# A hybrid decoder layer on one core: four large buffers instead of two, and another layout and loading order in the FFN's down phase

## The chip, the cores and the metric

The kernel runs on one core of one Trainium2 chip. The metric is the device time of one execution in microseconds (us); lower is better. Profile lines come from one profiled execution; engines are PE (matmul), PEld (its weight loads), DVE (VectorE), ACT (ScalarE), POOL (GpSimd) and SP (SyncE). DMAs are issued by SP, POOL and, for one small store, ACT, each into a queue of its own.

## The reference

One layer of a decoder on x of 1024 tokens by 1024 channels, all float32. Two token mixers run beside each other, then a gated FFN with a causal convolution of three taps. Cut to what matters:

```python
h = layer_norm(x, ln_in_g, ln_in_b)
u_glu, z, xbc, dt_raw, gate_a, gate_b = split_in(h @ w_in)
y_a = conformer_branch(u_glu, ...)       # GLU, causal conv of 31 taps, LN, silu, @ w_conv_out
y_b = ssd_branch(z, xbc, dt_raw, ...)    # conv of 4 taps, Mamba-2 SSD in chunks of 128, gated RMS norm, @ w_ssm_out
mix = (sigmoid(gate_a) * y_a + sigmoid(gate_b) * y_b) @ w_o
h = layer_norm(DN_ALPHA * h + mix, ln1_g, ln1_b)
u = causal_dwconv(h @ w_up, dw_w, dw_b)  # 1024 -> 2 * 2816 channels, 3 taps
gate, val = split(u)
ffn = (silu(gate) * val) @ w_down        # 2816 -> 1024
h = layer_norm(DN_ALPHA * h + ffn, ln2_g, ln2_b)
```

## The kernel before, in words

**Precision.** Every large matmul works on operands split in two: a high half (ACT casts to fp32r, a reduced-precision float that PE takes at full rate) and a low half (DVE subtracts the high half from the original). A product is three matmuls, high x high, high x low and low x high, which stand in `mm3` at L183, L184 and L185. So each weight tile of 128 x 1024 costs one ACT cast and one DVE subtraction before PE can use it: L149 and L154 in the mixers, L851/L852 in the up phase, L1116/L1117 in the down phase.

**Stages.** The tokens are done in two halves of 512 for the mixers (projections, the convolution of 31 taps as scalar_tensor_tensor operations on DVE at L466, the SSD chunks, the combination, the output projection). In the mixers' SSD branch a group's root mean square is found by a chain: a small PE product (L590), ACT's square root (L598), DVE's reciprocal (L599), a store to `nrm_scr` and a load back as `rstd`, and DVE's scaling with it (L605). Then comes the FFN over all 1024 tokens:

- *Up phase.* For each of 22 column blocks j, the 1024 x 1024 activations and the weights are taken as 2 x 2 blocks and multiplied with seven block products instead of eight (Strassen's scheme in Winograd's form), whose operands are called b11, b21, b22 and t1 to t4. `up_first` does b11 and b21; `up_rest` does t2, t3, t1, t4 and b22, brings the results from PSUM into `ug` and `uv` (ACT copies at L980, L983 and L988, DVE at L984 and L986; `fug`, `fuv` in the trace), runs the convolution of three taps (ACT L994, twice DVE L998 for each of gate and value), the silu (L1008) and the gating (L1009), and stores blocks and their differences to `b11_scr`, `b2_scr`, `t32_scr` and `t1_scr` (POOL, L1019 to L1027; the trace calls b11's and b2's both b_scr).
- *Down phase.* `down` is again seven block products, p = 0 to 6, each of 11 steps k. A step, `load(p, k)`, brings an activation block (SP, L1079) and a weight block (SP, L1082) into one raw buffer `dr` of five in a ring, for some products a further block `other` (POOL, L1088; `do` in the trace), forms the sums with a DVE addition (`add`, L1051: for p = 0 the sum is kept as `c3[k]`, for p = 1 as `c4[k]`), casts (L1116) and subtracts (L1117) into a weight buffer `w_dn`, and PE does 12 matmuls into four accumulators. After a product's last step its four accumulators are added to the residual rows `rs` (L1134 and its neighbours); when a row tile has both halves, its layer norm follows (L224, L238, L240, L244, L247) and its store. The last product runs its last eight steps one row tile after the other, so that the norms overlap it.

**Buffers.** SBUF is given out by pools with fixed numbers of buffers; an operation that needs a buffer waits until the last reader of its former content is done. Pool `big` has two buffers of 32 KiB per partition; they hold, one after the other, the transposed activations with their halves: `hT`, `yT`, `mixT`, then `h1b1` (b11 and b21) and `h1b2` (t3 and t4). In the down phase one holds the eight residual row tiles (`rows`) and the other the eleven c3 blocks; the weights of the last four steps of the last product (`last`) are built in c3's buffer at the end. The four `other` buffers are two pairs from two pools, taken in turn.

**Order.** The order of the instructions on each engine is set when the kernel is built: the Tile scheduler plays the program through with its own costs and gives each engine its list; `high_priority` moves a piece ahead, `issue_after` adds an order without a wait. On the chip each engine runs its list in order, and an instruction that waits holds up all behind it. An edit in one place can thus move instructions far from it.

## Time and profile before

| What | Value |
|---|---|
| runs | 1958.3, 1958.61, 1961.29 us; median 1958.61 |
| profiled execution | 1960.26 us, of which the span of the core's work is 1958.4 |
| TensorE's clock, mean over the span | 0.997 of full |
| busy, share of span | PE 99%, DVE 82%, PEld 80%, ACT 55%, POOL 11% |
| HBM traffic | 192 GB/s over the span |

PE's busy time says which engine sets the pace; since it is at 99%, one looks for the few places where PE waits, and at what released it. A line "PE ... [1.14 <-ACT w_dn L1116]" says that PE was idle for 1.14 us before that instruction and that ACT's instruction of line 1116 ended the wait. The table of stretches gives each engine's busy time between two times of the span, with the clock granted to PE, the share of time in which the 16 DMA engines were busy, and the rate. The chain is followed back from the last instruction to what released each step. For DMAs, "us to landing" counts from issue.

### The profile page before, as it was taken

Reading aid. Unit: us, or ns where it says so; the run is one execution under the profiler, and the core shown is the slowest. Engines: PE = TensorE matmul, PEld = TensorE weight load, DVE = VectorE, ACT = ScalarE, POOL = GpSimd, SP = SyncE. Lnnn points to the kernel's source line nnn. Section 1 sums busy time; section 2 is a strip of 40 time slices with the busy share of each in tenths; the row PEclk is TensorE's granted clock in tenths of the full one; section 3 lists DMA queues with packets and bytes.
Section 4 is the critical chain, followed back from the end, with each engine's and each line's share of the span. In section 5 each row is a group of like instructions: output and inputs, shape, how many; then the busy total and the mean of one; then the engine's idle time right before and its main releaser. Section 6 shows DMA issues by size and latency. Waiting matters only on the chain.

```text
span 1958.4 us, 25837 instructions
## 1 busy us (share of the span) xinstructions
PE 1929.1 (99%) x9453; PEld 1574.9 (80%) x9453; DVE 1599.8 (82%) x2224; ACT 1081.2 (55%) x1615; POOL 218.9 (11%) x258
## 2 busy tenths in 40 slices
PE   9999999999999999999999999999999999989997
PEld 8888878788788788888878888888888888867886
DVE  7599999999786538898999546587788888879778
ACT  4676767653263266777765435365555555544432
POOL 0001010112210001111112140010000000121010
PEclk9999999999999999999999999999999999999999
DMA  7645555447355565556545644566455455588673
GB/s 270 224 166 205 174 202 185 159 171 245 116 188 212 198 214 175 205 181 208 176 159 168 216 145 134 188 237 230 163 167 189 166 188 178 198 301 276 195 230 127
DMA packets 127648, 378.36 MB, mean 193 GB/s; under 512 B 15104, under 2 KB 15648, under 8 KB 127520
## 3 DMA queue, kind: packets, MB, share of 16 engines
q1 hardware_dynamic: 107424, 318.48, 48.2%
q0 software_dynamic: 13760, 46.69, 6.9%
q10 hardware_dynamic: 6336, 11.54, 1.6%
q8 instruction: 74, 1.21, 0.3%
q14 instruction: 54, 0.44, 0.1%
HBM read 289.99 MB, written 86.65 MB: 192 GB/s over the span
## 4 chain that ended last, share of the span: by engine, by line
PE 60%; DVE 10%; DMA 3%; ACT 2%; issue 2%; DVEq 0%; SPq 0%; ACTq 0%
PE acc L185 13%; PE acc L184 13%; PE acc L183 13%; PE sm L184 6%; PE sm L185 6%; PE sm L183 6%; DVE c L466 4%; DMA dr<-wdown 1%; DVE x L421 1%; DMA st_wo<-wo 1%; DMA b_scr<-fo 1%; PE sm L551 1%; PE sm L554 0%; DVE m L546 0%; ACT m L519 0%
## 5 line engine op out<-in xcount | busy, mean ns | idle before, releaser
L183 PE MATMUL acc<-hT,w_c 128*128 128x512 f32 x1000 | 391.2, 391 | 0.0
L185 PE MATMUL acc<-hT,w_c 128*128 128x512 f32 x1000 | 391.1, 391 | 0.0
L184 PE MATMUL acc<-hT,w_c 128*128 128x512 f32 x1000 | 391.0, 391 | 0.0
L466 DVE SCALAR_TENSOR_TENSOR c<-v,pc,c 128x512 f32<-128x512 f32 x480 | 369.7, 798 | 7.3 <-ACT c L455 4.5
L183 PEld LDWEIGHTS acc<-hT,w_c 128*128 128x128 f32 x1000 | 187.8, 188 | 40.6 <-issue 1.9
L185 PEld LDWEIGHTS acc<-hT,w_c 128*128 128x128 f32 x1000 | 187.8, 188 | 40.0 <-issue 1.5
L184 PEld LDWEIGHTS acc<-hT,w_c 128*128 128x128 f32 x1000 | 187.8, 188 | 39.5 <-issue 1.1
L149 ACT CAST w_c<-st_c 128x1024 fp32r<-128x1024 f32 x128 | 133.9, 1046 | 127.6 <-PE acc L185 100.6
L530 POOL TENSOR_TENSOR ce<-ce,xbc 128x1024 f32<-128x1024 f32 x28 | 82.2, 2936 | 681.7 <-ACT ce L529 681.7
L1116 ACT CAST w_dn<-dr 128x1024 fp32r<-128x1024 f32 (+1 forms) x73 | 68.6, 944 | 88.3 <-DMA dr<-wdown 36.7
L183 PE MATMUL sm<-h1s,w_s 128*128 128x512 f32 x264 | 102.7, 389 | 0.0
L184 PE MATMUL sm<-h1s,w_s 128*128 128x512 f32 x264 | 102.7, 389 | 0.0
L185 PE MATMUL sm<-h1s,w_s 128*128 128x512 f32 x264 | 102.2, 389 | 0.0
L519 ACT ACTIVATE m<-ab,acs 128x128 f32<-128x128 f32 x256 | 78.3, 390 | 37.7 <-PE sm L551 36.6
L154 DVE TENSOR_TENSOR w_c<-st_c,w_c 128x1024 fp32r<-128x1024 f32 x64 | 79.4, 1243 | 22.3 <-ACT w_c L149 17.1
L1117 DVE TENSOR_TENSOR w_dn<-dr,w_dn 128x1024 fp32r<-128x1024 f32 (+1 forms) x73 | 78.9, 1092 | 6.1 <-ACT w_dn L1116 6.1
L421 DVE SCALAR_TENSOR_TENSOR x<-u,pc,x 128x512 f32<-128x512 f32 x96 | 78.8, 835 | 3.9 <-ACT x L419 3.8
L185 PE MATMUL acc<-h1b,w_ue 128*128 128x512 f32 x176 | 68.8, 394 | 0.3 <-DVE w_ue L154 0.3
L183 PE MATMUL acc<-h1b,w_ue 128*128 128x512 f32 x176 | 68.7, 390 | 0.0
L184 PE MATMUL acc<-h1b,w_ue 128*128 128x512 f32 x176 | 68.5, 389 | 0.0
L183 PE MATMUL sm<-h1b,w_s 128*128 128x512 f32 x176 | 68.5, 389 | 0.0
L184 PE MATMUL sm<-h1b,w_s 128*128 128x512 f32 x176 | 68.5, 389 | 0.0
(325 smaller groups left out, 4547.3 us busy)
## 6 DMA issues: line engine op xcount, KB each, us to landing
st_c<-wcol SPq DMA_DIRECT2D x128, 512.0 KB, 4.4
low_scr<-w_c SPq DMA_DIRECT2D x64, 512.0 KB, 2.9
w_c<-low_scr SPq DMA_DIRECT2D x64, 512.0 KB, 4.4
ab<-acs_scr SPq DMA_DIRECT2D x32, 512.0 KB, 4.1
dr<-wdown SPq DMA_DIRECT2D x55, 256.0 KB, 5.2
st_wo<-wo SPq DMA_DIRECT2D x24, 512.0 KB, 4.5
st_ue<-wup SPq DMA_DIRECT2D x22, 512.0 KB, 3.6
first_scr<-first ACTq DMA_DIRECT2D x44, 256.0 KB, 3.0
```

The source lines that it names most:

```text
L149: casts.append(A.copy(w[:, 0, :], st))
L154: V.tensor_tensor(out=w[:, 1, :], in0=st, in1=w[:, 0, :].bitcast(F32), op=ALU.subtract)
L183: TE.matmul(ps, wa(0), xa(0), start=start, stop=False, skip_group_check=more)
L184: TE.matmul(ps, wa(0), xa(1), start=False, stop=False, skip_group_check=more)
L185: TE.matmul(ps, wa(1), xa(0), start=False, stop=stop, skip_group_check=more)
L421: V.scalar_tensor_tensor(out=o, in0=u[:, k : k + HALF], scalar=pc[:, wc + k : wc + k + 1], in1=o, op0=ALU.mult, op1=ALU.add,)
L466: V.scalar_tensor_tensor(out=accs[i], in0=v[:, k : k + HALF], scalar=pc[:, wc + k : wc + k + 1], in1=accs[i], op0=ALU.mult, op1=ALU.add,)
L519: A.activation(out=m[:, h, :], in_=ab[:, h, :], func=AF.Relu, scale=-1.0, bias=acs[:, c, 8 * g + h : 8 * g + h + 1],)
L530: G.tensor_tensor(out=ce, in0=ce, in1=CT[:, cs].unsqueeze(1).to_broadcast([P, 8, P]), op=ALU.mult)
L551: TE.matmul(o, xs[:, h * HP : (h + 1) * HP], m[:, h, :], start=True, stop=first)
L1116: A.copy(w[:, 0, cs], src)
L1117: V.tensor_tensor(out=w[:, 1, cs], in0=src, in1=w[:, 0, cs].bitcast(F32), op=ALU.subtract)
```

## The change

Nothing is computed in another way, and PE's matmuls stay the same in number. What changes is where things lie and when they are loaded:

1. Pool `big` has four buffers of 16 KiB instead of two of 32; an activation's high and low half are two tiles (`Parts` picks one by the first index).
2. In `down`, the four hold c3[0..7]; rows 0 to 3; c3[8..10] with c4[7] and c4[8]; and rows 4 to 7. Before, c3 took all of the buffer that `h1b2` leaves; now c3[0..7] and rows 0 to 3 take the two that `h1b1` leaves.
3. Rows 0 to 3 are loaded at the start of the phase; rows 4 to 7 in the third product (p = 2), behind the last `other` of the second; the norm's gain and offset rows (`ln2_g`, `ln2_b`) in the fifth (p = 4).
4. The four `other` buffers all come from one pool, and the last store of b11 is issued behind the fourth `other`. The weight buffer of step 3 is taken early (`first_own`).
5. The weights of the last four steps of the last product are built in the fifth product, one each at k = 3, 5, 7 and 9, into c3's two buffers.

```diff
-    big = ctx.enter_context(tc.tile_pool(name="big", bufs=2))
+    big = ctx.enter_context(tc.tile_pool(name="big", bufs=4))
...
     def big_tile(name):
-        return big.tile([P, 2, KD, HALF], F32R, tag="big", name=name)
+        return Parts(big.tile([P, KD, HALF], F32R, tag="big", name=f"{name}_{i}") for i in "hl")
...
-            G.dma_start(b11_scr[j], ov[:, early])
+            stores.append(G.dma_start(b11_scr[j], ov[:, early]))
...
-        rows, kept = flat_big("rows"), flat_big("c3")
-        c3 = [kept[:, k * HALF : (k + 1) * HALF] for k in range(NK)]
-        c4 = [dp.tile([P, HALF], F32, name=f"c4_{k}") for k in range(NK - 1)]
+        c3, rows03 = blocks(flat_big("c3")), flat_big("rows03")
+        more_c3 = blocks(flat_big("more_c3"))
+        c3 += more_c3[:3]
+        rows47 = flat_big("rows47")
+        c4 = [
+            more_c3[k - 4] if 7 <= k < 9 else dp.tile([P, HALF], F32, name=f"c4_{k}")
+            for k in range(NK - 1)
+        ]
...
-        for t in range(8):
-            G.dma_start(rs[t], h1_scr[t * P : (t + 1) * P, :])
-        g, b = (row(dp, w, D, n, eng=G) for w, n in ((RW_2G, "ln2_g"), (RW_2B, "ln2_b")))
+        first_own = dp.tile([P, 2, D], F32R, tag="w", bufs=3, name="w_dn_own")
+
+        def load_row(t):
+            i = G.dma_start(rs[t], h1_scr[t * P : (t + 1) * P, :])
+            if t >= 4:
+                issue_after(i, others[-1])
+
+        for t in range(4):
+            load_row(t)
...
-                    n_other += 1
-                    pl, tag = ((dp, "other"), (upp, "s"))[n_other % 2]
-                    other = pl.tile([P, HALF], F32, tag=tag, bufs=2, name=f"do{p}_{k}")
-                    G.dma_start(other, o_of)
+                    other = dp.tile([P, HALF], F32, tag="other", bufs=4, name=f"do{p}_{k}")
+                    others.append(G.dma_start(other, o_of))
+                    if len(others) == 4:
+                        issue_after(stores[-1], others[-1])
...
                     if not last:
-                        last.append(big_tile("last").rearrange("p i k t -> p (i k t)"))
-                    w = last[0][:, (k - NK + 4) * 2 * D : (k - NK + 5) * 2 * D]
-                    w = w.rearrange("p (i n) -> p i n", i=2)
+                        w = flat_big(f"last{k}", F32R)
+                        w = w.rearrange("p (j i n) -> p j i n", j=2, i=2)
+                        last.extend(w[:, j] for j in range(2))
+                    kept[k] = w = last.pop(0)
...
                 w = load(p, k)
+                if p == 2 and k % 2 and k < 8:
+                    load_row(4 + k // 2)
+                elif p == 4 and k == 1:
+                    load_norm()
+                elif p == 4 and k % 2:
+                    load(6, NK - 4 + k // 2 - 1)
...
-            ws = {k: load(p, k) for k in range(end, NK)}
+            ws = {k: kept.get(k) or load(p, k) for k in range(end, NK)}
```

Lines are shifted in the changed kernel: L1116/L1117 are L1148/L1149, L1051 is L1081, L1046 is L1066, L1088 is L1116, L994 is L1002, L998 is L1006, L984 and L986 are L992 and L994, L1009 is L1017, L1134 is L1166, L244 and L247 are L250 and L253, L599 is L605, L605 is L611.

The instructions move at four places. First POOL at the turn from the up to the down phase, before (`rows` are the residual rows, `do_` the `other` blocks of p = 0, b_scr and t_scr the stores of the up phase):

```order
175 L1046 DMA rows<-h_scr 128x1024 x8
176 L971 MEMSET fuv_14026 128x2
...
180 L1026 DMA t_scr_180<-fo_13955 128x1024
181 L1088 DMA do_0_14268<-wdown 128x512
182 L971 MEMSET fuv_14130 128x2
183 L1019 DMA b_scr_148<-fo_14104 128x512
184 L1088 DMA do_1_14289<-wdown 128x512
185 L1088 DMA do_3_14331<-wdown 128x512
186 L220 DMA ln_g<-prow 128x1024
187 L220 DMA ln_b<-prow 128x1024
188 L1088 DMA do_2_14310<-wdown 128x512
```

and the same place of the changed kernel:

```order
175 L1066 DMA rows_14243<-h_scr 128x1024 x4
176 L979 MEMSET fuv_14036 128x2
...
180 L1034 DMA t_scr_180<-fo_13965 128x1024
181 L979 MEMSET fuv_14140 128x2
182 L1116 DMA do_0_14273<-wdown 128x512
183 L1116 DMA do_1_14294<-wdown 128x512
184 L1116 DMA do_2_14315<-wdown 128x512
185 L1116 DMA do_3_14336<-wdown 128x512
186 L1027 DMA b_scr_148<-fo_14114 128x512
187 L1116 DMA do_4_14356<-wdown 128x512
```

Four row loads instead of eight stand at the start, the four first `other` loads are together and ahead of the last b11 store, and the norm's rows are gone from here.

DVE over the same turn, before: the last taps of the FFN's convolution (L998), the first weights' low halves (L1117) and the first sums (L1051).

```order
1726 L1117 TENSOR_TENSOR w_dn_0_14271<-dr_14265,w_dn_0_14271 128x1024
1727 L998 SCALAR_TENSOR_TENSOR fo_14100<-fug_14025,pc,fo_14100 128x1024
...
1729 L998 SCALAR_TENSOR_TENSOR fo_14100<-fug_14025,pc,fo_14100 128x1024
1730 L1117 TENSOR_TENSOR w_dn_1_14292<-dr_14286,w_dn_1_14292 128x1024
1731 L998 SCALAR_TENSOR_TENSOR fo_14104<-fuv_14026,pc,fo_14104 128x1024
1732 L984 TENSOR_TENSOR fuv_14130<-sm_14137,fuv_14130 128x512
1733 L1009 SCALAR_TENSOR_TENSOR fo_14104<-fo_14104,pc,fo_14100 128x1024
1734 L1117 TENSOR_TENSOR w_dn_2_14313<-dr_14307,w_dn_2_14313 128x1024
...
1737 L1051 TENSOR_TENSOR c_14233<-dr_14265,do_0_14268 128x512
```

and of the changed kernel:

```order
1726 L1006 SCALAR_TENSOR_TENSOR fo_14110<-fug_14035,pc,fo_14110 128x1024
1727 L1149 TENSOR_TENSOR w_dn_0_14276<-dr_14270,w_dn_0_14276 128x1024
...
1729 L1006 SCALAR_TENSOR_TENSOR fo_14114<-fuv_14036,pc,fo_14114 128x1024 x2
1730 L992 TENSOR_TENSOR fuv_14140<-sm_14147,fuv_14140 128x512
1731 L1017 SCALAR_TENSOR_TENSOR fo_14114<-fo_14114,pc,fo_14110 128x1024
1732 L1149 TENSOR_TENSOR w_dn_1_14297<-dr_14291,w_dn_1_14297 128x1024
1733 L1149 TENSOR_TENSOR w_dn_2_14318<-dr_14312,w_dn_2_14318 128x1024
1734 L1149 TENSOR_TENSOR w_dn_own<-dr_14333,w_dn_own 128x1024
1735 L1081 TENSOR_TENSOR c_14242<-dr_14270,do_0_14273 128x512
```

The first weight's low half now stands behind the first tap, the second's behind all taps and the gating, and the first sum follows the fourth low half. On PE the up phase's last products, b22 and t4 of block 21, stand behind the second weight's twelve matmuls before; now b22 stands ahead of the second weight's four high matmuls, and t4 between these and its other eight.

DVE at the end of the program, before (row tiles 6 and 7 of the layer norm):

```order
1972 L238 BN_AGGR mv_f_15908<-st_f_14251 128x2
1973 L1134 SCALAR_TENSOR_TENSOR rows<-rows,acc_14227 128x512
1974 L244 SCALAR_TENSOR_TENSOR rows<-rows,mv_f_15908,ln_g 128x512 x2
1975 L240 RECIPROCAL rs_f_15909<-rs_f_15909 128x1
1976 L224 BN_STATS st_f_14252<-rows 128x6
1977 L247 SCALAR_TENSOR_TENSOR rows<-rows,rs_f_15909,ln_b 128x512 x2
```

and of the changed kernel:

```order
1970 L244 BN_AGGR mv_f_15919<-st_f_14261 128x2
1971 L250 SCALAR_TENSOR_TENSOR rows_14245<-rows_14245,mv_f_15919,ln_g 128x512 x2
1972 L246 RECIPROCAL rs_f_15920<-rs_f_15920 128x1
1973 L1166 SCALAR_TENSOR_TENSOR rows_14245<-rows_14245,acc_14237 128x512
1974 L253 SCALAR_TENSOR_TENSOR rows_14245<-rows_14245,rs_f_15920,ln_b 128x512 x2
1975 L230 BN_STATS st_f_14262<-rows_14245 128x6
```

The pair that subtracts row tile 6's mean (L244, now L250) moves ahead of the addition of the last accumulator.

And DVE in the first half's mixers, before (convolution taps, weights' low halves w_c_46 and w_c_47, the reciprocal of the fourth group):

```order
571 L154 TENSOR_TENSOR w_c_46_4391<-st_c_46_4389,w_c_46_4391 128x1024
572 L466 SCALAR_TENSOR_TENSOR c_6_4222<-v_6_3506,pc,c_6_4222 128x512
573 L599 RECIPROCAL rows_3_4204<-rows_3_4204 128x128
574 L466 SCALAR_TENSOR_TENSOR c_7_4224<-v_7_3574,pc,c_7_4224 128x512
...
578 L154 TENSOR_TENSOR w_c_47_4425<-st_c_47_4423,w_c_47_4425 128x1024
```

and of the changed kernel:

```order
567 L472 SCALAR_TENSOR_TENSOR c_7_4227<-v_7_3576,pc,c_7_4227 128x512
568 L605 RECIPROCAL rows_3_4207<-rows_3_4207 128x128
569 L472 SCALAR_TENSOR_TENSOR c_6_4225<-v_6_3508,pc,c_6_4225 128x512
570 L472 SCALAR_TENSOR_TENSOR c_7_4227<-v_7_3576,pc,c_7_4227 128x512
571 L160 TENSOR_TENSOR w_c_46_4394<-st_c_46_4392,w_c_46_4394 128x1024
```

The reciprocal stands five rows earlier, ahead of w_c_46's low half instead of behind it, by the scheduler's choice alone; the source there is the same.

More of the change, by code (lines that the diff above doesn't have):

```diff
@@ L52, with __getitem__ @@
 CT_N = 72
+class Parts(tuple):
+    def __getitem__(self, at):
+        return tuple.__getitem__(self, at[1])[(at[0], *at[2:])]
 @with_exitstack
@@ L957, in up_weights @@
         return w24, w10, w3
+    stores = []
     def up_rest(upp, bl, j, before):
@@ L1034, in down, with flat_big, blocks, load_norm @@
         X, Y = [bank(1) for _ in range(4)], [bank(0) for _ in range(4)]
[L1036 to L1041 removed]
+        def flat_big(name, dtype=F32):
+            t = big.tile([P, KD, HALF], dtype, tag="big", name=name)
+            return t.rearrange("p k t -> p (k t)")
+        def blocks(t):
+            return [t[:, k * HALF : (k + 1) * HALF] for k in range(KD)]
+        c3, rows03 = blocks(flat_big("c3")), flat_big("rows03")
[6 more added lines that the diff above has]
+        ]
         c4.append(upp.tile([P, HALF], F32, tag="s3", name="c4_last"))
[L1043 removed]
+        rs = [r[:, t * D : (t + 1) * D] for r in (rows03, rows47) for t in range(4)]
         sts = [dp.tile([P, 2, 6], F32, name=f"st_f{t}") for t in range(8)]
[L1045 to L1047 removed]
+        g, b = (dp.tile([P, D], F32, name=n) for n in ("ln2_g", "ln2_b"))
+        first_own = dp.tile([P, 2, D], F32R, tag="w", bufs=3, name="w_dn_own")
[5 more added lines that the diff above has]
+            load_row(t)
+        def load_norm():
+            for r, start in ((g, RW_2G), (b, RW_2B)):
+                i = G.dma_start(r, prow[start : start + D].partition_broadcast(P))
+                issue_after(i, others[-1])
         E, L = slice(0, HALF), slice(HALF, D)
@@ L1051, in add @@
             V.tensor_tensor(out=dst, in0=x, in1=y, op=ALU.add)
[L1053 removed]
+        n_steps, n_raw = 0, 0
         def raw(name):
@@ L1059, in raw @@
             return pl.tile([P, D], F32, tag=tag, bufs=bufs, name=f"{name}_{n_raw}")
-        last = []
+        last, others, kept = [], [], {}
         def load(p, k):
-            nonlocal n_steps, n_other
+            nonlocal n_steps
             a11, a21, a12, a22 = (wdown[h * NK + k, :, cs] for h in range(2) for cs in (E, L))
```

7 lines of the change are left out of this document (2 added, 5 removed).

## The prediction

> **What bounds the kernel now.** I read the table of engines first, then PE's waits by stretch, PE's timeline where it waits, the chain that ended last around those places, and a table of stretches.
>
> ```profile
> PE 1929.1 (99%) x9453; PEld 1574.9 (80%) x9453; DVE 1599.8 (82%) x2224; ACT 1081.2 (55%) x1615; POOL 218.9 (11%) x258
> ```
>
> TensorE is the bound: of a span of 1958.4 us it is idle 1958.4 - 1929.1 = 29.3 us. The change takes away no matmul, so it can win only from these 29.3 us, or add to them. PE's waits in 500:520, 990:1000 and 1700:1800 (us in total, times, longest):
>
> ```profile
> PE acc L185 <- DVE w_gb L154: 4.2, 1, 4.2
> ...
> PE sm L551 <- DVE m L546: 2.5, 1, 2.5
> ...
> PE acc L184 <- DVE w_dn L1117: 3.7, 3, 1.6
> PE sm L184 <- DVE w_dn L1117: 2.1, 1, 2.1
> PE acc L183 <- ACT w_dn L1116: 2.1, 2, 1.1
> ```
>
> So 4.2 us stand in the first half's mixers and 7.9 us at the start of the down phase, all waits for weights being prepared. PE's timeline there (start, duration, idle time before in brackets):
>
> ```profile
> 1726.62 1.19 PE L183 MATMUL acc<-w_dn 128*128 128x512 f32 x4 [1.14 <-ACT w_dn L1116]
> 1729.09 0.50 PE L184 MATMUL acc<-w_dn 128*128 128x512 f32 x1 [1.28 <-DVE w_dn L1117]
> ...
> 1745.74 1.20 PE L183 MATMUL acc<-w_dn 128*128 128x512 f32 x4 [0.92 <-ACT w_dn L1116]
> ...
> 1754.61 0.50 PE L184 MATMUL acc<-w_dn 128*128 128x512 f32 x1 [1.62 <-DVE w_dn L1117]
> ...
> 1761.18 0.50 PE L184 MATMUL acc<-w_dn 128*128 128x512 f32 x1 [0.80 <-DVE w_dn L1117]
> ...
> 1774.70 0.50 PE L184 MATMUL sm<-w_dn 128*128 128x512 f32 x1 [2.09 <-DVE w_dn L1117]
> ```
>
> They add to 7.85 us. What they hang on, in the chain (start, us, what):
>
> ```profile
> 1710.47 12.35 DMA b_scr<-fo
> ...
> 1727.90 1.15 DVE w_dn L1117
> ...
> 1736.44 0.24 PE sm L185
> 1736.70 0.70 DVE c L1051
> 1737.84 6.74 DMA dr<-wdown
> ...
> 1754.95 11.95 DMA dr<-wdown
> ```
>
> Two causes show. A store of the convolved block takes 12.35 us beside the burst of eight row loads; the FFN's last DVE work starts late behind it, and the low half of the second weight ends only at 1729.05. Then the first sum into c3 waits for the last up product (PE's end at 1736.68), since c3 lies in that product's operand; the raw buffers that feed the sums are held till then, SP's next load goes out at 1737.8 and lands at 1744.6, and the gaps from 1745 on follow. The stretches (length, then busy us of PE, PEld, DVE, ACT, POOL, then PE's granted clock, DMA share, GB/s):
>
> ```profile
> 425.00:510.00 85.00, 80.78 (x383) 65.26 (x382) 82.80 (x109) 34.62 (x46) 18.89 (x17) 0.99 0.56 189
> ...
> 512.00:514.00 2.00, 2.00 (x6) 1.63 (x5) 1.97 (x4) 0.00 (x0) 0.00 (x0) 0.50 0.98 350
> ...
> 996.00:998.00 2.00, 0.86 (x16) 0.89 (x18) 2.00 (x4) 1.98 (x3) 0.00 (x0) 1.00 0.48 193
> ...
> 1725.00:1800.00 75.00, 67.10 (x287) 52.64 (x286) 67.05 (x82) 31.38 (x32) 17.01 (x32) 1.00 0.83 289
> 1797.00:1858.00 61.00, 61.00 (x270) 50.50 (x270) 47.33 (x66) 29.21 (x40) 3.29 (x6) 1.00 0.63 202
> 1858.00:1918.00 60.00, 60.00 (x266) 49.69 (x265) 45.46 (x58) 24.62 (x29) 6.56 (x12) 1.00 0.68 216
> 1920.00:1940.00 20.00, 20.00 (x90) 16.57 (x89) 20.00 (x40) 5.67 (x11) 0.00 (x0) 1.00 0.29 107
> 1948.00:1958.00 10.00, 0.17 (x1) 0.00 (x0) 7.21 (x15) 0.59 (x2) 0.00 (x0) 0.68 0.43 158
> ```
>
> A matmul costs 60.00/266 = 0.226 us; the twelve of one down step about 2.72. After 1800 PE has no idle time until its last matmul at 1948.17; from there DVE finishes alone.
>
> **The change part by part.** *Four row loads ahead of the store, and the first weights (1.14 + 1.28).* ACT's timeline of before:
>
> ```profile
> 1718.31 0.58 ACT L988 COPY fug<-sm 128x512 f32<-128x512 f32 x1
> ...
> 1722.98 1.15 ACT L994 ACTIVATE fo<-fug,pc 128x1024 f32<-128x1024 f32 x1 [1.85 <-DMA b_scr<-fo]
> ```
>
> The scaling L994 needs `fug`, there at 1718.9, and a buffer that the store gives back at 1722.8. With four rows the burst is 2 MiB instead of 4, and half of it has gone when the store is issued; if the store lands in six us (the row load on SP's queue beside it, shown below, took 6.4), L994 starts at 1718.9, four us sooner, and DVE's work behind it too. PE's order now puts the b22 and t4 products between the first weight and the lows of the second: 24 matmuls, 5.4 us of cover. That low half goes behind one tap, one subtraction and one multiplication more on DVE, about 3.0 together: 1729.05 - 4 + 3 = 1728. PE asks for it at 1725.5 + 0.7 + 5.4 + 0.9 = 1732.5. The 0.7 is a new wait that I expect: b22 adds to a bank that ACT copies first, about 1726. What speaks against it: the first weight's cast and low half now stand behind L994 and the first tap. If the store stays at 12.35, the cast ends at 1722.98 + 2.1 = 1725.1 and the low at 1726.6, where PE wants them at 1722.6 and 1723.5: 3.1 us of new waits in place of 2.42. Gain 1.7, bounds 2.42 and -0.7.
>
> *c3 in the early buffers (0.92 + 1.62 + 0.80 + 2.09 = 5.43).* c3[0..7] now lies where h1b1 was, whose last product is long over, and four `other` loads are issued back to back ahead of the last b11 store. The first sum is then bounded by DVE's own queue: three lows from 1728, about 1732 to 1733 in place of 1736.7, so SP's ring turns 4 us sooner: w_dn_5 could be cast at about 1744.6 - 4 = 1740.6, and PE wants it, without the earlier gaps, at about 1742. Also 3 MiB leave this stretch (rows 4 to 7, and two norm rows of 0.5 MiB each), where the DMA engines are busy 0.83 of the time and a load took 11.95. What is late next is DVE: it has 67.05 us to do here, and if the stretch shrinks by 7 us that is 67.05 of 68. The low halves that come closest have some 1 to 2 us of slack in my walk through the new order, so I leave 0.6 of gaps. Gain 4.8; bounds 5.43, and zero if DVE's queue holds the sums as long as c3's buffer did.
>
> Together 6.5, bounds -0.7 and 7.85.
>
> *The loop of four `other` buffers* replaces two pairs that were taken in turn, four in all as well. Its DMA rows in 1700:1800 (KB each, median us to landing):
>
> ```profile
> do<-wdown POOLq DMA_DIRECT2D x26, 256.0 KB, 5.7
> ...
> rows<-h_scr POOLq DMA_DIRECT2D x8, 512.0 KB, 10.4
> ...
> fug<-first_scr SPq DMA_DIRECT2D x1, 256.0 KB, 6.4
> ```
>
> At 5.7, with the sum's 0.70 and about 0.5 for the issue, a buffer turns in 6.9, four give one per 1.73 us: below the 2.72 of a step. Cost 0.
>
> *Rows 4 to 7, norm rows.* They go out on POOL's queue behind the last `other` of the second product. POOL is busy 3.29 of 61 us in 1797:1858 and no row is wanted before the last product. The DMA engines moved 202 GB/s there; 3 MiB over 61 us add 52, giving 254, less than the 289 that 1725:1800 carried. Cost 0, up to 4 if the burst delays SP's loads (a rival below).
>
> *Last weights built in the fifth product.* Four weights, each two half-casts on ACT and two half-lows on DVE (about 0.6 each) and one load on SP, move there from the last product. DVE is busy 45.46 of 60 us in 1858:1918; plus 4.8 makes 50.3. Covered by PE, cost 0; without that cover, 4.8 at most. The place they leave is DVE's full stretch 1920:1940.
>
> *The tail.* DVE's rows after PE's end:
>
> ```profile
> 1948.21 0.69 DVE L1134 SCALAR_TENSOR_TENSOR rows<-rows,acc 128x512 f32<-128x512 f32 x1
> 1948.81 1.41 DVE L244 SCALAR_TENSOR_TENSOR rows<-rows,mv_f,ln_g 128x512 f32<-128x512 f32 x2
> ...
> 1953.88 1.41 DVE L247 SCALAR_TENSOR_TENSOR rows<-rows,rs_f,ln_b 128x512 f32<-128x512 f32 x2
> ```
>
> The L244 pair of row 6 stands ahead of the last L1134 in the new order: 1950.14 - 1948.81 = 1.33 us less to do after PE. DVE has room to do it, since the last weights' lows are gone. Gain 1.33, bounds 1.33 and 0.
>
> *The gap at 509.* The scheduler also moves a square-root chain of the first half:
>
> ```profile
> 461.21 0.95 DVE L599 RECIPROCAL rows<-rows 128x128 f32<-128x128 f32 x1
> ...
> 472.73 2.74 DVE L605 SCALAR_TENSOR_TENSOR x<-x,pc,rstd 128x512 f32<-128x512 f32 x4 [1.77 <-DMA rstd<-nrm_scr]
> ...
> 509.67 0.80 PE L185 MATMUL acc<-hT,w_gb 128*128 128x512 f32 x1 [4.22 <-DVE w_gb L154]
> 510.26 0.63 PE L183 MATMUL acc<-hT,w_gb 128*128 128x512 f32 x1
> 510.69 0.63 PE L184 MATMUL acc<-hT,w_gb 128*128 128x512 f32 x1
> ```
>
> DVE is busy 82.80 of 85 us in 425:510; the 1.77 is most of what it idles, and everything behind it up to PE's wait is DVE's queue. The reciprocal now stands one weight low and several taps sooner, about 3 us, more than 1.77, and what it goes through (a store and a load back) shifts along. So DVE no longer waits, and PE's gap falls to 4.22 - 1.77 = 2.45. After the gap, 512:514 still ran at clock 0.50; matmuls start 0.43 us apart instead of 0.226, 11 of them up to 514.4: 2.2 us. After the 2.5 us gap at 997, the clock was 1.00. So I count 2.2 as gained too. Bounds 0 and 3.97.
>
> The Trainium skill ("TensorE: Matmul & The Clock Gate", section "🔬 Part 1: The HAM clock gate (the "warmup" mystery)") says that the clock falls to half after an idle window of 3.4 us, and that the window runs freely. The trace agrees: 0.50 behind 4.22, 1.00 behind 2.5. By that rule a gap of 2.45 cannot fill a window, and the 2.2 us go for certain.
>
> **Sum.** The profiled execution took 1960.26 us, 1.86 outside its span. 1960.26 - 6.5 - 1.33 - 1.77 - 2.2 = 1948.5. The three runs shown have median 1958.61, 1.65 less than the profiled one; those near 1958.3 may have had no half clock. Then 1958.61 - 6.5 - 1.33 - 1.77 = 1949.0. I take 1948.8.
>
> **The rivals.** *Partial: DVE becomes the bound at the start of down, or the store stays long.* For it: 67.05 us of DVE work in a stretch that would last 68. Against it: a steady step asks of DVE 1.15 + 2 x 0.6 = 2.35, under 2.72. If half of the 6.5 stay: 1948.8 + 3.3, about 1952 to 1953.
>
> *The gap at 509 stays*, if DVE's 1.77 only turns into waiting elsewhere: 1958.61 - 7.83 = 1950.8, or 1952.4 against the profiled run.
>
> *The burst of rows 4 to 7 stalls SP's loads.* For it: the store of 12.35 us beside the eight rows, whose median was 10.4. Against it: the load on SP's queue in that stretch took 6.4. A raw buffer turns every five steps, 13.6 us, of which some 3 are work; a load above 10 us costs. At 12.35 for two of them: +4, about 1953.
>
> The Trainium skill ("DMA: Bandwidth & Descriptors", section "🔬 Queues, rings and completion order") says that each DMA engine takes turns between queues by packet. It speaks against 3 MiB at once on POOL's queue, which would get as much as SP's loads while they last. The trace agrees that SP's loads suffer less than what queues on POOL's side (6.4 beside 12.35), so that by the page the stall is small.
>
> *Slower: the loop of four.* If an `other` takes L to land, a step takes (L + 1.2)/4, which passes 2.72 at L = 9.7. To lose the 10 us gained and 4 more over the 22 steps that use it takes 0.64 a step, L = 12.2, as long as the store took under the row burst. Time then 1962.6 and up. Against it: 5.7 measured with more traffic about. It decides only if the loads of both products are all that slow.
>
> *The change does nothing where it aims*: if the gaps only move, 1958.61 - 1.33 = 1957.3.
>
> **How the numbers follow.** 0.2% of 1958.61, 3.9 us, is about what can be told from no change: 1954.7 and 1962.5. Chances: forecast 0.58 (1946 to 1951.5); gap at 509 stays 0.10; half of the down gaps stay 0.18 (a fifth of it above 1954.7); stall by the rows 0.05; nothing 0.05; loop of four 0.04. Faster 0.58 + 0.10 + 0.15 + 0.04 = 0.87, same 0.09, slower 0.04. The range: at the low end all of 7.85, 1.33 and the whole 4.22 go, 1958.61 - 13.4 = 1945.2; at the high end half the down gaps and the gap at 509 stay, 1952.5 to 1954.5. I give 1945 to 1955.
>
> **What would show it.** Right: PE's idle time in 1720:1780 under 1.5 us; a c3 sum before the last up product ends; the b_scr store under 8 us; no wait of DVE for rstd near 470, PE's gap there about 2.4 with clock 1.00 behind it; 5.7 us of DVE after PE's last matmul. Wrong: waits of PE for DVE with DVE busy without a break from 1725 to 1760; raw loads over 10 us in the third product; sums that wait for an `other`.

## The result, and the profile after

The changed kernel takes 1951.83 us (median of six executions, 1950.19 to 1953.2); the kernel before took 1961.32 in the six executions beside them (1958.3 to 1967.26). The ratio is 0.995, 95% interval 0.994 to 0.996: some 9.5 us faster, where 9.8 were forecast. The profiled execution took 1951.93 us, its span 1950.2 against 1958.4 before, 8.2 us less.

The table of engines: PE does the same work in the shorter span.

```profile
PE 1928.1 (99%) x9453; PEld 1575.1 (81%) x9453; DVE 1601.4 (82%) x2224; ACT 1080.5 (55%) x1615; POOL 219.8 (11%) x258
```

PE's timeline at the places where it still waits (start, duration, idle time before in brackets):

```profile
509.34 0.50 PE L191 MATMUL acc<-hT_h,w_gb 128*128 128x512 f32 x1 [2.40 <-DVE w_gb L160]
...
1724.02 0.50 PE L189 MATMUL sm<-h1s,w_s 128*128 128x512 f32 x1 [0.52 <-ACT fuv L991]
...
1793.11 1.20 PE L189 MATMUL acc<-w_dn 128*128 128x512 f32 x4 [0.78 <-ACT w_dn L1148]
1795.41 0.80 PE L190 MATMUL acc<-w_dn 128*128 128x512 f32 x1 [1.11 <-DVE w_dn L1149]
1796.01 0.63 PE L191 MATMUL acc<-w_dn 128*128 128x512 f32 x1
1796.43 0.63 PE L190 MATMUL acc<-w_dn 128*128 128x512 f32 x1
```

The six waits of before at 1726 to 1775, 7.85 us, have become one of 0.52, the new wait for ACT's copy that was forecast at 0.7. But two waits stand where PE had none, 1.89 us near 1794, and the matmuls behind them start 0.43 us apart instead of 0.226. Stretches of the changed kernel (length, busy us of PE, PEld, DVE, ACT, POOL, then granted clock, DMA share, GB/s):

```profile
508.00:512.00 4.00, 2.66 (x12) 2.21 (x13) 4.00 (x5) 0.00 (x0) 2.14 (x1) 1.00 0.40 122
...
1720.00:1780.00 60.00, 59.48 (x263) 48.92 (x262) 58.32 (x69) 27.52 (x28) 18.04 (x34) 1.00 0.86 300
1780.00:1830.00 50.00, 48.11 (x205) 39.10 (x204) 40.97 (x58) 22.68 (x31) 1.87 (x4) 0.97 0.72 240
1830.00:1900.00 70.00, 69.71 (x307) 57.15 (x306) 51.84 (x67) 27.79 (x33) 9.60 (x18) 1.00 0.75 243
```

The gap at 509 has shrunk to 2.40 and the clock behind it is 1.00, as forecast. In 1780:1830 the clock is 0.97, where it was 1.00 before, and 1830:1900 shows a small wait of 0.29. At the tail, DVE from its last accumulator to its last operation:

```profile
1941.32 0.69 DVE L1166 SCALAR_TENSOR_TENSOR rows<-rows,acc 128x512 f32<-128x512 f32 x1 [0.94 <-PE acc L191]
...
1945.74 1.42 DVE L253 SCALAR_TENSOR_TENSOR rows<-rows,rs_f,ln_b 128x512 f32<-128x512 f32 x2
```

From the last accumulator to the end it is 1950.2 - 1941.32 = 8.88 us, against 1958.4 - 1948.21 = 10.19 before.

### The profile page after: what moved, and what is told of

Read it like the earlier page. It is cut to its first block, busy times and chain, and to the rows that moved or that the text cites. A ratio compares the mean times of both kernels' runs of the same rounds, so it can differ in the third digit from the quotient of the medians.

```text
span 1950.2 us, 25837 instructions
## 1 busy us (share of the span) xinstructions
PE 1928.1 (99%) x9453; PEld 1575.1 (81%) x9453; DVE 1601.4 (82%) x2224; ACT 1080.5 (55%) x1615; POOL 219.8 (11%) x258
## 4 chain that ended last, share of the span: by engine, by line
PE 70%; DVE 19%; DMA 5%; ACT 3%; issue 3%; SPq 0%; DVEq 0%; ACTq 0%
PE acc L191 16%; PE acc L190 16%; PE acc L189 16%; DVE c L472 7%; PE sm L190 5%; PE sm L191 5%; PE sm L189 5%; DMA dr<-wdown 2%; DVE w_c L160 2%; DVE x L427 1%; DVE w_dn L1149 1%; DMA dr<-b_scr 1%; PE sm L557 1%; PE sm L560 1%; DMA c_scr<-c 1%
## 5 line engine op out<-in xcount | busy, mean ns | idle before, releaser
L191 PE MATMUL acc<-hT_h,w_c 128*128 128x512 f32 x1000 | 391.5, 392 | 0.5 <-DVE w_c L160 0.5
L189 PE MATMUL acc<-hT_h,w_c 128*128 128x512 f32 x1000 | 391.6, 392 | 0.0
L190 PE MATMUL acc<-hT_l,w_c 128*128 128x512 f32 x1000 | 391.3, 391 | 0.0
L191 PEld LDWEIGHTS acc<-hT_h,w_c 128*128 128x128 f32 x1000 | 187.8, 188 | 40.9 <-issue 1.5
L189 PEld LDWEIGHTS acc<-hT_h,w_c 128*128 128x128 f32 x1000 | 187.9, 188 | 40.7 <-issue 1.9
L190 PEld LDWEIGHTS acc<-hT_l,w_c 128*128 128x128 f32 x1000 | 187.8, 188 | 39.3 <-issue 1.1
L1148 ACT CAST w_dn<-dr 128x1024 fp32r<-128x1024 f32 (+1 forms) x72 | 67.4, 942 | 78.3 <-DVE dr L1081 44.6
L1149 DVE TENSOR_TENSOR w_dn<-dr,w_dn 128x1024 fp32r<-128x1024 f32 (+1 forms) x72 | 77.9, 1088 | 3.9 <-ACT w_dn L1148 3.8
L191 PE MATMUL acc<-h1b_h,w_ue 128*128 128x512 f32 x176 | 68.9, 395 | 0.0
L189 PE MATMUL acc<-h1b_h,w_ue 128*128 128x512 f32 x176 | 68.7, 390 | 0.0
L190 PE MATMUL acc<-h1b_l,w_ue 128*128 128x512 f32 x176 | 68.6, 390 | 0.0
L189 PE MATMUL sm<-h1b_h,w_s 128*128 128x512 f32 x176 | 68.5, 389 | 0.0
L190 PE MATMUL sm<-h1b_l,w_s 128*128 128x512 f32 x176 | 68.5, 389 | 0.0
```

Source lines behind the costliest of these rows:

```text
L189: TE.matmul(ps, wa(0), xa(0), start=start, stop=False, skip_group_check=more)
L190: TE.matmul(ps, wa(0), xa(1), start=False, stop=False, skip_group_check=more)
L191: TE.matmul(ps, wa(1), xa(0), start=False, stop=stop, skip_group_check=more)
L1148: A.copy(w[:, 0, cs], src)
L1149: V.tensor_tensor(out=w[:, 1, cs], in0=src, in1=w[:, 0, cs].bitcast(F32), op=ALU.subtract)
```

## The experiments

Times are medians; "before" beside them was 1961.4 to 1962.1 in all. Each kernel is the changed one with an edit, where nothing else is said. In the "expected" texts A and B are theories of that run alone.

**1. The burst of rows at the start of the down phase: burst8 and before4.** burst8 adds four loads:

```diff
+        for t in range(4):
+            G.dma_start(early[:, t * D : (t + 1) * D], h1_scr[t * P : (t + 1) * P, :])
         for t in range(4):
             load_row(t)
```

> Adds four loads of 512 KB ahead of the rows at the start of the down phase (into c3's buffer before its first use; nothing reads them), so the burst is 4 MiB as in the kernel before. Theory A: the store issued after it lands in 11 to 13 us instead of about 5, ACT's scaling and with it the cast of the first weight, which now stands behind it, come at about 1724, and PE waits 2.5 to 3.1 us for the first weight; the time rises by 2 to 3, to about 1954. Rival: the raw loads and the store share the DMA engines well enough; the store lands under 8 us, PE's wait stays at the 0.5 for ACT's copy and the time stays at 1951.8.

It took 1954.18 us. The row of the store behind the burst (KB, us to landing) in the changed kernel, then in burst8, then PE's timeline in burst8:

```profile
b_scr<-fo POOLq DMA_DIRECT2D x1, 512.0 KB, 6.8
```

```profile
b_scr<-fo POOLq DMA_DIRECT2D x1, 512.0 KB, 12.4
...
1727.56 1.20 PE L189 MATMUL acc<-w_dn 128*128 128x512 f32 x4 [1.13 <-ACT w_dn L1151]
1730.04 0.50 PE L190 MATMUL acc<-w_dn 128*128 128x512 f32 x1 [1.28 <-DVE w_dn L1152]
...
1760.74 1.20 PE L189 MATMUL sm<-w_dn 128*128 128x512 f32 x4 [0.48 <-ACT w_dn L1151]
```

The burst sets the store's landing, 6.8 or 12.4 us, and two waits as in the kernel before, 1.13 and 1.28, come back with it. A expected waits for the first weight; these are for the second: with eight loads the scheduler put b22 and t4 behind the second weight again, as in the kernel before. Number of rows and order of products go together. Of the later 5.43 us only 0.48 come back, though the burst is as large as before.

before4 is the kernel before with that part alone:

```diff
-        for t in range(8):
-            G.dma_start(rs[t], h1_scr[t * P : (t + 1) * P, :])
+        for t in range(4):
+            load_row(t)
...
+                if p == 2 and k % 2 and k < 8:
+                    load_row(4 + k // 2)
```

> The kernel before with one part of the change: rows 0 to 3 loaded at the start of the down phase, rows 4 to 7 behind the last other load of the second product; everything else as before. Theory A (two causes): the store lands under 8 us, the 2.42 us of PE's waits at 1726 and 1729 fall to about 0.5, the waits of 5.4 us between 1745 and 1775 stay, and a wait near 1793 of 1 to 2 us comes; time 0 to 2 us under the kernel before. Theory B (the burst is all): the waits between 1745 and 1775 go too, under 1.5 us; time 5 to 7 us under the kernel before, about 1955.

It took 1962.35, ratio to before 0.9999 (0.999 to 1.0008). PE's timeline:

```profile
1726.41 0.50 PE L183 MATMUL sm<-h1s,w_s 128*128 128x512 f32 x1 [0.52 <-ACT fuv L983]
...
1747.74 0.50 PE L184 MATMUL acc<-w_dn 128*128 128x512 f32 x1 [0.51 <-DVE w_dn L1124]
1753.61 0.55 PE L184 MATMUL acc<-w_dn 128*128 128x512 f32 x1 [2.41 <-DVE w_dn L1124]
...
1801.58 0.70 PE L184 MATMUL acc<-w_dn 128*128 128x512 f32 x1 [2.29 <-DVE w_dn L1124]
1809.78 0.50 PE L184 MATMUL acc<-w_dn 128*128 128x512 f32 x1 [0.46 <-DVE w_dn L1124]
```

The first two waits fall from 2.42 to 0.52 here too, and of the later 5.43 us 2.92 stay; but 2.75 stand near 1800, where the rows are now loaded and the kernel before had none. Alone, this part wins nothing.

**2. Where c3 lies: c3_late.**

```diff
-        c3, rows03 = blocks(flat_big("c3")), flat_big("rows03")
-        more_c3 = blocks(flat_big("more_c3"))
+        more_c3, rows03 = blocks(flat_big("more_c3")), flat_big("rows03")
+        c3 = blocks(flat_big("c3"))
```

> Only the placing is turned round: c3[0..7] lies in a buffer that h1b2 leaves (the last up product's operand) and c3[8..10] with two c4 blocks in one that h1b1 leaves; loads and their order in the program are as in the changed kernel. Theory A: what was won at the start of the down phase is c3 being free before the last up product ends. Then the first sum into c3 waits for the last t4 matmul again, PE's waits between 1735 and 1780 come back with 4 to 5.5 us in all, and the time is 1956 to 1957. Rival: the smaller burst of row loads and the grouped other loads did it, and DVE is the limit; then PE waits for less than 1.5 us there and the time is 1951 to 1952.5.

It took 1952.25, and PE has no wait between 1725 and 1790. But this edit moves nothing: in the built program c3[0..7] has the same address as in the changed kernel, where the high half of `h1b1` was, and every instruction, its place in the order and its waits are the same. The order of these lines in the source doesn't decide here which buffer a tile gets. The trace shows it too. In c3_late, PE's last t4 matmul and DVE's first sum, then the first sum of the changed kernel:

```profile
1730.18 0.39 PE L191 MATMUL sm<-h1b_h,w_s 128*128 128x512 f32 x1
...
1730.34 0.68 DVE L1081 TENSOR_TENSOR c<-dr,do 128x512 f32<-128x512 f32 x1
```

```profile
1730.44 0.69 DVE L1081 TENSOR_TENSOR c<-dr,do 128x512 f32<-128x512 f32 x1
```

The sum begins while the t4 matmul still runs; from a buffer that t4 reads it would have had to wait. So c3_late is the changed kernel measured four more times, and decides neither for A nor for its rival. A kernel that differs in c3's place alone was not run.

What other traces show of c3's place: the first sum in the kernel before, in burst8, and in pairs (experiment 3):

```profile
1736.70 1.29 DVE L1051 TENSOR_TENSOR c<-dr,do 128x512 f32<-128x512 f32 x2 [0.41 <-PE sm L185]
```

```profile
1737.14 0.68 DVE L1084 TENSOR_TENSOR c<-dr,do 128x512 f32<-128x512 f32 x1
```

```profile
1724.47 0.68 DVE L1081 TENSOR_TENSOR c<-dr,do 128x512 f32<-128x512 f32 x1
```

In the kernel before, DVE sat idle for only 0.41 us until t4's end let the first sum go; up to then its own queue held the sum. In burst8 c3 lies early, the first sum comes as late as before, and 0.48 us of the later waits return. In pairs c3 lies early, the first sum comes seven us before t4 is done, and 3.17 return. So by these traces the time of the first sum does not set these waits; c3's place alone stays untested.

**3. The `other` loads: pairs and other2.** pairs takes two pairs of buffers in turn again, with the b11 store ahead of the second load and the norm rows between the loads:

```diff
-                    other = dp.tile([P, HALF], F32, tag="other", bufs=4, name=f"do{p}_{k}")
+                    pl, tag = ((upp, "s"), (dp, "other"))[len(others) % 2]
+                    other = pl.tile([P, HALF], F32, tag=tag, bufs=2, name=f"do{p}_{k}")
...
+                    if len(others) == 2:
+                        issue_after(others[-1], stores[-1])
+                        for i in norm_rows:
+                            issue_after(i, others[-1])
```

> The changed kernel with the other loads as they were before the change: two pairs of buffers taken in turn, the last b11 store ahead of the second other load, and the two norm rows loaded between the other loads at the start of the down phase. Rows, c3 and the last weights stay as changed. Theory A: after c3_late, it is the four other loads standing together, ahead of the store and without the norm rows, that let the first sums come early; then the third or fourth sum waits for its other load again, and PE's waits between 1735 and 1785 come back with 3 to 5.4 us; time 1955 to 1957. Theory B: the four rows instead of eight alone brought the whole start of the down phase forward; then PE waits for less than 1.5 us there and the time is 1951 to 1952.5.

It took 1956.44, ratio to before 0.9971 (0.9961 to 0.9981). POOL and PE in pairs:

```profile
1729.57 0.55 POOL L1027 DMA_DIRECT2D b_scr<-fo  x1 [5.91 <-DVE fo L1017]
1730.11 1.10 POOL L1121 DMA_DIRECT2D do<-wdown  x2
...
1749.50 1.20 PE L189 MATMUL acc<-w_dn 128*128 128x512 f32 x4 [1.76 <-ACT w_dn L1157]
1752.10 0.79 PE L190 MATMUL acc<-w_dn 128*128 128x512 f32 x1 [1.41 <-DVE w_dn L1158]
```

The second and third `other` go out behind the store at 1730.11, where the changed kernel issues all four from 1723.06; the second sum then comes at 1734.68 instead of 1731.65, and 3.17 us of waits return in the place of the 5.43, with a clock of 0.94 over 1720:1780. So at least these waits went because the four loads stand together, ahead of the store and without the norm rows; which of the three counts, pairs doesn't separate. The smaller burst alone takes some 2.5 of the 5.43 (before4), and with the loads together the large burst brings back only 0.48 (burst8): the two overlap, and the order of the `other` loads is the larger part.

other2 leaves two buffers of four (`bufs=2`).

> Two other buffers instead of four (and the last b11 store behind the second). A step's buffer turns in landing plus 1.2 us; with loads of 6.5 us that is 7.7, over two buffers 3.85 a step against PE's 2.72. Theory A: the loop of these buffers sets the pace: 22 steps lose up to 1.1 us each less what the start hides, 15 to 25 us, so 1967 to 1977, with DVE's sums waiting for other loads. With this the point at which four would bind, 9.7 us of landing, is confirmed. Rival: loads land faster when fewer are in flight (about 4 us), the loop turns in 2.6 a step and nothing is lost beyond 2 us.

It took 1963.69, 12 us more than the changed kernel, less than the 15 to 25 of A. Its loads' row in 1722:1812 and PE's longest waits:

```profile
do<-wdown POOLq DMA_DIRECT2D x24, 256.0 KB, 4.6
...
1794.52 0.80 PE L190 MATMUL acc<-w_dn 128*128 128x512 f32 x1 [1.89 <-DVE w_dn L1149]
1804.84 0.80 PE L190 MATMUL acc<-w_dn 128*128 128x512 f32 x1 [3.14 <-DVE w_dn L1149]
```

With fewer in flight a load lands in 4.6 instead of 5.7 us, so two buffers give a step per (4.6 + 1.2)/2 = 2.9, just above 2.72. By this estimate 22 steps lose 4 us; PE's waits in 1730:1830 add up to 7.5, and six or seven matmuls at half clock follow each of the two longest. So the direction fits, the size does not, and where the rest comes from stays open. A chain of four at 5.7, 1.7 a step, has room.

**4. The late rows: norows and rows_sp.** norows fills rows 4 to 7 by a memset instead of loads:

```diff
             if t >= 4:
+                i = G.memset(rs[t], 1.0)
                 issue_after(i, others[-1])
```

rows_sp loads them, and the norm rows, on SP's queue, one row per second step:

```diff
-            i = G.dma_start(rs[t], h1_scr[t * P : (t + 1) * P, :])
+            with tc.high_priority(offset=4000):
+                i = SY.dma_start(rs[t], h1_scr[t * P : (t + 1) * P, :])
+            issue_after(i, raws[-1])
```

> Leaves out the loads of residual rows 4 to 7 (2 MiB on POOL's queue near 1773 us; POOL fills those rows with a constant instead, so the last half of the output is not the reference's). Theory A: PE's two waits of the changed kernel near 1793 (0.78 and 1.11 us) and the half clock behind them (about 8 matmuls at 0.43 instead of 0.226 us, 1.6) come from that burst, which delays the raw loads of the third product. Then both waits fall under 0.3 us, the clock stays 1.00 to 1800, the raw loads land in under 7.5 us, and the time falls by 3 to 3.5 to about 1948.5. Theory B: DVE's own work bunches there (sums into c4, row sums and norm statistics at the turn of two products); then both waits stay within 0.3 us of what they were and the time stays at about 1951.8.

> Rows 4 to 7 and the two norm rows go out on SP's queue, one behind the raw load of every second step of the third product (rows) and behind the second step of the fifth (norm rows), instead of back to back on POOL's. Theory A (the burst stalls the raw loads): spread out, the waits near 1793 fall to under 0.5 us together and the time falls by 2.5 to 3.5, to about 1949. Theory B (DVE's own bunching): the waits stay, 1951.8. A third way: each 512 KB row now stands in front of a raw load on the same queue and delays it by 1.3 to 2 us, so new waits of about 0.5 to 1 us each come at the odd steps of the third product, and the time is 1950 to 1953.

norows took 1950.36, rows_sp 1948.95, ratios to before 0.9948 (0.9931 to 0.9964) and 0.9938 (0.9923 to 0.9953). The burst in the changed kernel, first on POOL and then a raw load beside it in the chain (start, us):

```profile
1773.30 2.13 POOL L1066 DMA_DIRECT2D rows<-h_scr  x4
...
1777.99 0.54 POOL L1075 DMA_DIRECT2D ln_g<-prow  x1
1781.05 0.54 POOL L1075 DMA_DIRECT2D ln_b<-prow  x1 [2.52 <-issue]
...
1775.24 9.43 DMA dr<-wdown
```

The raw loads in 1770:1800, in the changed kernel and in norows, and PE in 1780:1830 of norows:

```profile
dr<-wdown SPq DMA_DIRECT2D x10, 256.0 KB, 8.3
```

```profile
dr<-wdown SPq DMA_DIRECT2D x11, 256.0 KB, 4.7
...
1780.00:1830.00 50.00, 50.00 (x221) 41.11 (x220) 43.39 (x62) 23.85 (x33) 1.10 (x2) 1.00 0.66 211
```

The same loads in rows_sp, and PE's waits there:

```profile
dr<-wdown SPq DMA_DIRECT2D x11, 256.0 KB, 5.4
...
1753.93 1.20 PE L189 MATMUL sm<-w_dn 128*128 128x512 f32 x4 [0.89 <-ACT w_dn L1152]
...
1798.49 0.50 PE L190 MATMUL acc<-w_dn 128*128 128x512 f32 x1 [0.74 <-DVE w_dn L1153]
```

Without the loads, PE is never idle there and the clock stays full: theory A. The whole time falls by only 1.5 us, since a wait of 1.39 comes at 1830:1900 in norows, for which see experiment 5. With the rows spread on SP's queue the raw loads land in 5.4 us, and the wait of 1.89 near 1794 becomes one of 0.74 at 1798, with another of 0.89 at 1754. It takes the whole burst: norows still sends the two norm rows there, and pairs sends rows 4 to 7 without them (its raw loads land in 6.3 us), and in neither does PE wait between 1780 and 1830. That pairs runs three us later at this place may have a part in it.

**5. The last weights: last_late**, built in the last product again:

```diff
-                elif p == 4 and k % 2:
-                    load(6, NK - 4 + k // 2 - 1)
```

> Builds the weights of the last four steps of the last product in the last product again, as the kernel before did; all else as changed. Theory A: the tail's 1.3 us were won because DVE had room to take row 6's subtraction before the last accumulator; in this kernel's order that pair stands behind it again, so DVE has 7.0 us to do after PE's last matmul instead of 5.7 and the time rises by 1.3 to about 1953, with no new PE wait. Rival: DVE is full in the last 30 us, the lows delay the row tiles further and PE waits for accumulators: over 2.5 us more. Second rival: the early build cost as much as it won (more DVE work in the fifth product, PE's wait of 0.3 us there); then the time stays at 1951.8.

It took 1951.05, no more than the changed kernel. Its stretch 1830:1900, and DVE's last accumulator and last operation:

```profile
1830.00:1900.00 70.00, 70.00 (x311) 57.98 (x310) 51.73 (x66) 28.29 (x32) 9.84 (x18) 1.00 0.73 233
...
1941.85 0.69 DVE L1166 SCALAR_TENSOR_TENSOR rows<-rows,acc 128x512 f32<-128x512 f32 x1
...
1947.52 1.42 DVE L253 SCALAR_TENSOR_TENSOR rows<-rows,rs_f,ln_b 128x512 f32<-128x512 f32 x2
```

The tail is 1952.0 - 1941.85 = 10.15, so the 1.3 us of the tail do come from the early build. But the early build has a price that I put at 0: it takes raw buffers and loads in the fifth product, and PE waits for the sixth's weights near 1890. In the ten profiles of kernels with it that wait is between 0 and 2.83 us (0.29, 1.93 and 0 in the three of the changed program: its own, after_again and c3_late); in the four without it (before, before4, recip_only, last_late) there is none. Three of the ten have none either, so one profile doesn't show the price. The second rival is the one that the time bears out: as much is paid as won, within what four executions can tell.

**6. The gap at 509: recip_only and recip_back.** Both tie one DVE operation; recip_only is the kernel before:

```diff
+    def tie():
+        if (0, 3) in recips and "c0_46" in lows:
+            issue_after(lows["c0_46"], recips.pop((0, 3)))
```

> The kernel before with one thing forced: the same reciprocal stands ahead of the low half of weight 46. Theory A: that alone takes DVE's wait of 1.77 for rstd, PE's gap at 509 falls from 4.22 to about 2.4 to 3, the clock stays 1.00 behind it, and the time falls by 2 to 4 against the kernel before on the same chip; the down phase's 7.9 us of waits stay. Rival: no change at 509 beyond 0.3 us, and the time of before.

> The changed kernel with one thing forced: the reciprocal of the fourth group in the first half stands behind the low half of weight 46 again (2.5 us of DVE work later). Theory A: DVE then waits for rstd again, about 1 to 1.8 us near 472, PE's gap at 509 grows from 2.40 to 3.4 to 4.2, and if it passes the point the clock falls to half behind it for some 11 matmuls (2.2 us): time up by 1 to 4, to 1953 to 1956. Rival: the gap's length comes from elsewhere in DVE's queue; gap 2.4 and time 1951.8.

recip_only took 1958.48, ratio 0.9986 (0.9977 to 0.9995), that is 2.7 us faster than before; recip_back took 1953.7, ratio 0.9959 (0.9944 to 0.9974), about 2 slower than the changed kernel in the medians, with intervals that overlap. PE's gap in recip_only, with the stretch behind it, then DVE's scaling and PE's gap in recip_back:

```profile
508.18 0.50 PE L193 MATMUL acc<-hT,w_gb 128*128 128x512 f32 x1 [2.01 <-DVE w_gb L160]
...
508.00:512.00 4.00, 3.82 (x10) 3.04 (x11) 3.97 (x6) 0.00 (x0) 1.28 (x1) 0.59 0.68 218
```

```profile
472.85 2.74 DVE L620 SCALAR_TENSOR_TENSOR x<-x,pc,rstd 128x512 f32<-128x512 f32 x4 [1.99 <-DMA rstd<-nrm_scr]
...
509.79 0.72 PE L199 MATMUL acc<-hT_h,w_gb 128*128 128x512 f32 x1 [4.40 <-DVE w_gb L166]
```

The place of the reciprocal sets the gap, 2.0 or 4.4: DVE's wait for `rstd`, 1.77 before, is gone in recip_only and in the changed kernel, and in recip_back it is there again with 1.99. The clock does not follow the gap's length: behind 2.01 it fell to half, behind 2.40 in the changed kernel it did not.

**7. Both repairs, and the changed kernel again: best and after_again.** best is rows_sp with the sums of c4 and c3 held back:

```diff
-                    add(c4[k], c4[k], c3[k])
+                    issue_after(add(c4[k], c4[k], c3[k]), halves_low[2, k])
```

> The kernel with rows 4 to 7 and the norm rows on SP's queue, and in addition the sums c4 + c3 of the fourth product ordered behind the low half of the same step of the third product, so that DVE does them when it has room. If DVE's bunching has a part in the waits that were left near 1755 and 1798 (0.89 and 0.74), these fall under 0.4 us each, and the time is about 1947 to 1948, 1 to 2 under rows_sp's 1949 and 4 under the changed kernel. If they come from slow loads alone, the time stays at 1949.

> The changed kernel once more, beside the others on the same chip. The same waits at the same places (0.5 near 1724, 0.8 and 1.1 near 1793); PE's gap at 509 at 2.2 to 2.5 us. With a gap of that length the clock behind it was 1.00 in three profiles and 0.59 to 0.77 in five, so either is possible here; if the half clock comes only in some executions, it explains a spread of about 2 us among its runs. Median 1951 to 1952.5.

after_again took 1951.35 (ratio 0.9949, 0.9935 to 0.9962), best 1953.76 (0.9953, 0.9941 to 0.9966). In best's profile PE has no wait but the 0.52 between 1720 and 1880, so by these two profiles DVE's bunching had a part in what was left there; but it waits later:

```profile
1890.43 0.50 PE L190 MATMUL sm<-w_dn 128*128 128x512 f32 x1 [1.13 <-DVE w_dn L1155]
1895.15 0.50 PE L190 MATMUL sm<-w_dn 128*128 128x512 f32 x1 [1.70 <-DVE w_dn L1155]
```

The 1.63 us that were won at 1754 and 1798 are more than given back in the sixth product, behind the early weights. That the held-back sums cause this is not shown: the same wait is 0 to 1.93 in three executions of the changed program. No version here is shown to beat the changed kernel: rows_sp is lowest, but its interval overlaps. rows_sp with the last weights built late is what the runs point to; it wasn't tried.

## Why the prediction was right, and where not

Against the profiled execution the sum was 11.8 us (6.5 + 1.33 + 1.77 + 2.2); measured were 8.3.

- *Start of the down phase, 6.5 with 0.52 to 0.7 left.* The waits there fell by 7.85 - 0.52 = 7.3. The part of the store and the first weights went as worked out: it landed in 6.8 (six assumed), ACT's scaling started at 1716.94 right behind `fug`, the new wait is 0.52 (0.7). For the 5.43 the size was right (4.8 forecast) and the main cause was not: I put it to c3's early buffer, which had held DVE for 0.41 us in the kernel before. By burst8 and pairs the larger part was the four `other` loads standing together, which the prediction mentions in a half-sentence and prices only as a loop. That the size came out is luck in this respect.
- *Rows 4 to 7 at cost 0.* This step failed. The sum of average rates, 254 GB/s, hid that 3 MiB go out within 10 us: the raw loads' median rises to 8.3 us, one takes 9.43, DVE falls behind at the turn of two products, and PE loses 1.89 us, then some seven matmuls at half clock, 7 x 0.2 = 1.4. The rival had the mechanism and nearly the price (4), with a chance of 0.05 that was too low; it asked for loads above 10 us, and shorter ones were enough.
- *The page on queues.* The Trainium skill ("DMA: Bandwidth & Descriptors", section "🔬 Queues, rings and completion order") has the engines take turns between queues by packet; from that I read a small stall. The trace bears out the direction, and the raw loads at 8.3 instead of 4.7 us show that a fair share is not enough for a stage which needs most of the rate.
- *The early weights at cost 0.* They cost 0 to 2.8 us near 1890. DVE's room, busy 45 of 60 us, was counted; the raw buffers and the loads were not.
- *The tail, 1.33.* Measured 10.19 - 8.88 = 1.31, and last_late gives it back.
- *The gap at 509, 4.22 to 2.45.* Measured 2.40, with the reason shown by recip_only and recip_back.
- *The clock behind it, 2.2 "for certain".* It came so in the profiled execution, but this step is refuted as an argument. Of eleven profiles with a gap between 2.0 and 2.6 us there, four kept the clock at 1.00 (2.38, 2.40, 2.43, 2.49) and seven fell to 0.59 to 0.82 over 508:512 (2.01 to 2.61). The Trainium skill ("TensorE: Matmul & The Clock Gate", section "🔬 Part 1: The HAM clock gate (the "warmup" mystery)") lets the clock fall after an idle window of 3.4 us; here gaps of 2.0 us are enough, and the measurement decides.

The rest of the difference is outside the change: before 490 us PE idles 0.8 us more in the changed kernel's profile than in that of before, and the 14 profiles range from 3.4 to 5.0 there.

Against the profiled execution this closes: 3.3 near 1794, 0.3 near 1890 and 0.8 before 490, less the 0.8 more that was won at the start of the down phase, make 3.6, and the sum was 11.8 - 8.3 = 3.5 too high. The median is 3.0 us above the forecast. That the difference between the kernels still came out nearly as forecast, 9.5 against 9.8, is luck: the kernel before took 1961.32 in the median of six executions, and not 1958.61 as in the three that were known.

## What to carry to other kernels

A load that is wanted much later is not free because the stage's mean rate has room: spread it, one piece per step, or it delays the loads that feed the bound engine. When a chain of waits is removed, price each supposed cause by the idle time that it ends: here the buffer that the chain named had cost DVE 0.41 us, and the place of four loads on one queue counted for more. And an edit that is to move a buffer must show the wait that goes with it: c3_late's edit changed no instruction. Work that moves to an idle stretch of an engine also takes buffers and queue places there; count these as well as the engine's time.

## What the hardware showed that was not expected

The clock's fall is not decided by the length of one gap. At 509, gaps of 2.01, 2.20, 2.24, 2.33, 2.52 and 2.61 us were followed by half clock, and 2.38, 2.40 and 2.43 were not; 2.49 came once with it and once without. Waits of 0.78 and 1.11 us, 1.2 us apart near 1794, were followed by a stretch at 0.50:

```profile
1796.00:1798.00 2.00, 2.00 (x6) 1.62 (x5) 1.90 (x3) 0.54 (x1) 0.00 (x0) 0.50 0.87 281
```

while 1.22 and 1.11 at the same place in after_again, the same program, were not, nor 1.14 and 1.28 near 1727 in the kernel before; and the gap of 2.5 us near 995 left the clock at 1.00 in all 14 profiles. Why this last gap never does it and the one at 509 often does stays open. With eleven matmuls at 0.43 instead of 0.226 us a fall costs about 2.2 us by estimate, which can make a part of the spread between executions of the same program (1949.25 to 1955.72 in the five of after_again); that it does is not shown.
